# Attention scores from stacked rows of 128 built by DMA, with transposes and values moved further behind the scores

## The chip, the cores and the metric

The kernel runs on one core of one Trainium2 chip. The metric is the device time of one execution in microseconds (us), median of several runs. PE is TensorE, DVE is VectorE, ACT is ScalarE, POOL is GpSimd, SP is SyncE, which issues the DMAs.

## What is computed

A decoder trunk of two layers on a sequence of 256 tokens, width 1024, all in float32: softmax attention (16 heads of 64, partial rotary, causal inside one block of 256 tokens) and a SwiGLU feed-forward, then an mLSTM mixer (8 heads) and a second SwiGLU. Pre-norms and residual adds stand around each part. The change touches the attention alone:

```python
q = partial_rotary(qkv[0], cos, sin)
k = partial_rotary(qkv[1], cos, sin)
s_own = jnp.einsum('bhqd,bhkd->bhqk', qc, k_own, preferred_element_type=jnp.float32)
s_own = jnp.where(kpos[None, :] <= qpos[:, None], s_own, -jnp.inf)
p = jax.nn.softmax(jnp.concatenate([s_sel, s_own], axis=-1), axis=-1)
o = p @ v                                   # per head, then through w_o
```

## The kernel before

Every float32 operand is split into a high part (rounded to fp32r) and a low part (the rest), and a product is three fp32r matmuls: high by high, high by low, low by high. Weights come from HBM in units of 128x1024 (`raw`, 4 buffers), ACT casts the high part (`wh`, L150), DVE subtracts the low part (`wl`, L141).

The attention works on eight pairs of heads, hp 0 to 7. A pair goes through this chain:

- **qk**: 48 matmuls of 256 columns on PE into one PSUM bank (`pair_block`; pairs 0 and 1 come from the stage ahead). **rotary** (L473): DVE shuffles the bank into `sh` and multiplies it into `qk`, which ends the use of the bank; POOL multiplies `sh` and adds it to `qk`.
- **split_qk** (L486): ACT casts `qk` to the high half of `u`, DVE subtracts for the low half. In `u` the 64 dimensions of the pair's first head lie on partitions 0 to 63, those of the second on 64 to 127.
- **scores** (L514): 12 matmuls that contract over 64 rows, in turn for the first and the second head, into two PSUM banks.
- **softmax, exps, recip, normalize** for each head: DVE masks and takes the row maximum (`mx`, L532) and so frees the scores' bank, ACT takes the exponential (L538), DVE the reciprocal, ACT scales (`p`, L550).
- **transposes** (L555): three 128x128 transposes per head into a bank; ACT casts `ph` (L566), DVE subtracts `pl` (L569).
- **values** (L575): 12 matmuls per pair, then ACT casts `oh` (L590) and DVE subtracts `ol` (L594). The output projection `ao` reads both.

All these share four PSUM banks (`ps`); the value projection `av` and `ao` accumulate in four others (`acc`).

The order of PE, DVE and ACT in this stage is written out by the class `Stream`: it walks a list of generators (qk of pair 2, half of av, qk 3, rest of av, qk 4 to 7, then ao), each yield is one step, 92 steps in all, and a step is six matmuls of 256 columns or three of 512. Between steps it emits what is due by a position. For pair hp with s0 = `A_PAIR[hp]`, `split_qk` is due at s0 + `A_U`, the scores at s0, the transposes at s0 + `A_T`, the values at s0 + `A_V`; the pieces of the softmax follow each other by half a step to one and a half. What isn't ready in program order (`when`) is put off by half a step. The engines then run their own queues in the order of emission, so an instruction that waits holds up all behind it on its engine. The mLSTM stage has a helper, `stacks` (L434 and following), that this stage does not call: it makes `u` and copies it by six DMAs on SP into `stk`, in which a head's high and low rows lie on one set of 128 partitions, so that `dots` (L455) gets the three products out of two matmuls that contract over 128 rows.

Of the kernel before, what the change touches and what calls it, by code (L numbers as in the profile page):

```python
# [9 lines left out]
F32 = mybir.dt.float32  # L10
F32R = mybir.dt.float32r
# [5 lines left out]
P = 128  # L17
S = 256
# [8 lines left out]
LAG = 6  # L27
WARM = 16

A_PAIR = (9, 18, 27, 36, 48, 57, 65, 73)  # L30
A_U, A_T, A_V, A_W = -4, 6, 12, 1
M_START, M_STEP, M_A, M_B, M_C, M_G2, M_G3 = 32, 5, 1.5, 12, 22, 23, 28


# [33 lines left out]
def trunk_kernel(ctx: ExitStack, tc: tile.TileContext, x, w, wg, fw, tab, out):  # L68
    nc = tc.nc
# [25 lines left out]
    def ps_tile():  # L95
        return ps_pool.tile([P, 512], F32, name="ps", tag="ps")
# [79 lines left out]
    def mm(o, lhsT, rhs, start, stop):  # L176
        nc.tensor.matmul(o, lhsT=lhsT, rhs=rhs, start=start, stop=stop, skip_group_check=True)  # L177
# [96 lines left out]
    def tok_block(name, i0, n, evict, later):  # L274

        banks = [acc_tile() for _ in range(2)]
        for k in range(NF):
            if k % 2 == 0:
                u = unit(name, i0 + k // 4, k // 2 % 2)
            for t in range(2):  # L280
                wh, wl = (a[:, (k % 2) * 512:(k % 2 + 1) * 512] for a in u)
                mm3(banks[t], n.xt(k, t), (wh, wl), k == 0, k == NF - 1)
                yield
        later(evict, i0 // 2, banks)

    class Stream:
# [13 lines left out]
        def later(self, d, f, *args):  # L300
            self.at(self.pos + d, f, *args)
# [42 lines left out]
    def out_steps(acc, name, i, src):  # L344

        u, rhs = unit(name, i // 2, i % 2), src.pop(i)
        for b in range(4):
            out_tiles(acc, u, rhs, False, False, fs=(2 * b, 2 * b + 1))
            yield

    def out_start(acc, name, src):

        steps = []
        for bs in ((0, 1), (2, 3)):
            acc.extend(acc_tile() for _ in bs)
            for i in range(2):
                if bs[0] == 0:
                    steps.append((unit(name, 0, i), src.pop(i)))
                u, rhs = steps[i]
                for b in bs:  # L360
                    out_tiles(acc, u, rhs, i == 0, False, fs=(2 * b, 2 * b + 1))
                    yield
# [71 lines left out]
    def stacks(pool, mv, bufs, ubufs=2, later=None):  # L434


        u = pool.tile([P, 1024], F32R, name="u", tag="u", bufs=ubufs)
        nc.scalar.copy(u[:, 0:512], mv)
        st = pool.tile([P, 2, 768], F32R, name="stk", tag="stk", bufs=bufs)

        def rest():
            nc.vector.tensor_sub(u[:, 512:1024], mv, u[:, 0:512].bitcast(F32))
            for hh in range(2):
                r = slice(hh * 64, hh * 64 + 64)
                nc.sync.dma_start(out=st[0:64, hh].bitcast(F32), in_=u[r, 0:768].bitcast(F32))
                nc.sync.dma_start(out=st[64:128, hh, 0:512].bitcast(F32), in_=u[r, 512:1024].bitcast(F32))
                nc.sync.dma_start(out=st[64:128, hh, 512:768].bitcast(F32), in_=u[r, 0:256].bitcast(F32))

        if later is None:
            rest()  # L450
        else:
            later(rest)
        return st

    def dots(o, T, a0, na, m0, nm):  # L455
        a = T[:, 256 + a0:256 + a0 + na]
        mm(o, a, T[:, m0:m0 + nm], True, False)
        mm(o, a, T[:, 512 + m0:512 + m0 + nm], False, True)

    with ExitStack() as actx:  # L460
        ap = actx.enter_context(tc.tile_pool(name="attn", bufs=3))
# [9 lines left out]
        rq = {}  # L471
# [9 lines left out]
            nc.gpsimd.tensor_add(qk, qk, sh)  # L481
            rq[hp] = qk

        us = {}

        def split_qk(hp):  # L486

            qk = rq.pop(hp)
            u = ap.tile([P, 1024], F32R, name="u", tag="u", bufs=3)
            nc.scalar.copy(u[:, 0:512], qk)  # L490

            def low_u():
                nc.vector.tensor_sub(u[:, 512:1024], qk, u[:, 0:512].bitcast(F32))
                us[hp] = u
            main.later(1.5, low_u)

        evicted = set()

# [13 lines left out]
                evicted.add(i)  # L512

        def scores(hp):  # L514

            u = us.pop(hp)
            sc = [ps_tile() for _ in range(2)]
            for o, a0, nm in ((0, 0, P), (P, P, S)):
                for i, (al, ml) in enumerate(((0, 0), (0, 1), (1, 0))):
                    for hh in range(2):  # L520
                        r = slice(hh * 64, hh * 64 + 64)
                        mm(sc[hh][:, o:o + nm], u[r, al * 512 + S + a0:al * 512 + S + a0 + P],
                           u[r, ml * 512:ml * 512 + nm], i == 0, i == 2)
            for hh in range(2):
                main.later(0.5 + hh, softmax, 2 * hp + hh, sc[hh])

# [19 lines left out]
        pr = {}  # L546
# [5 lines left out]

        pT = {}

        def transposes(h):  # L555
            pt = pr.pop(h)
            tp = ps_tile()

            for i in range(3):
                nc.tensor.transpose(tp[:, i * P:(i + 1) * P], pt[:, i * P:(i + 1) * P], ident)  # L560
            main.later(1, halves, h, tp)

        def halves(h, tp):
            ph = ap.tile([P, 384], F32R, name="ph", tag="ph", bufs=4)
            pl = ap.tile([P, 384], F32R, name="pl", tag="pl", bufs=4)
            nc.scalar.copy(ph, tp[:, 0:384])  # L566

            def low_p():
                nc.vector.tensor_sub(pl, tp[:, 0:384], ph.bitcast(F32))  # L569
                pT[h] = (ph, pl)  # L570
            main.later(1, low_p)
# [3 lines left out]
        def values(hp):  # L575

            po = ps_tile()
            for hh in range(2):
                p = pT.pop(2 * hp + hh)
                for s, c, q in ((0, 0, 0), (1, S, P)):  # L580
                    for i, (vl, pl) in enumerate(((0, 0), (0, 1), (1, 0))):
                        mm(po[0:64, hh * S + q:hh * S + S], VT[:, s, 2 * hp + hh, vl * 64:vl * 64 + 64],
                           p[pl][:, c:c + S - q], hh == 0 and s == 0 and i == 0, s == 1 and i == 2)
            oh = ap.tile([P, S], F32R, name="oh", tag="oh", bufs=8)
            ol = ap.tile([P, S], F32R, name="ol", tag="ol", bufs=8)
            parts = [(slice(hh * 64, hh * 64 + 64), po[0:64, hh * S:hh * S + S]) for hh in range(2)]

            def high_o():
                for r, o in parts:
                    nc.scalar.copy(oh[r], o)  # L590

            def low_o():
                for r, o in parts:
                    nc.vector.tensor_sub(ol[r], o, oh[r].bitcast(F32))  # L594
                ot[hp] = (oh, ol)
            main.later(1, high_o)
            main.later(2, low_o)

        def qk(hp):
            b = ps_tile()  # L600
            yield from pair_block("aqk", hp, n, b)
            main.later(1, rotary, hp, b)
# [3 lines left out]
        main = Stream(*[(always, g) for g in (qk(2), islice(vb, 8), qk(3), vb, qk(4), qk(5), qk(6), qk(7))],  # L606
                      ((lambda: 0 in ot and 1 in ot), out_start(acc, "ao", ot)), *[((lambda hp=hp: hp in ot), out_steps(acc, "ao", hp, ot)) for hp in range(2, 7)])
        for hp in range(2):
            main.at(0, rotary, hp, banks[hp])
        main.at(0.5, v_evict, 0, banks[2:4])  # L610
        for hp, s0 in enumerate(A_PAIR):
            main.when(s0 + A_U, lambda hp=hp: hp in rq, split_qk, hp)
            main.when(s0, lambda hp=hp: hp in us, scores, hp)
            for hh in range(2):
                main.when(s0 + A_T + hh, lambda h=2 * hp + hh: h in pr, transposes, 2 * hp + hh)
            main.when(s0 + A_V, lambda hp=hp: 2 * hp in pT and 2 * hp + 1 in pT and hp // 4 in evicted, values, hp)
        with tc.manual_schedule(engines=vector_scalar):
            wlag[0], look[0] = A_W, A_LOOK
# [73 lines left out]
    with ExitStack() as mctx:  # L692
# [179 lines left out]
        def o_evict(i, banks):  # L872
# [3 lines left out]
            for t in range(2):  # L876
# [5 lines left out]
        main = Stream((always, tok_block("mv", 0, n, v_evict2, lambda *a: main.later(0, *a))), (always, tok_block("mo", 0, n, o_evict, lambda *a: main.later(0, *a))),  # L882
                      (always, tok_block("mv", 2, n, v_evict2, lambda *a: main.later(0, *a))), (always, tok_block("mo", 2, n, o_evict, lambda *a: main.later(0, *a))),
                      ((lambda: 0 in yt and 1 in yt), out_start(acc, "mout", yt)), *[((lambda h=h: h in yt), out_steps(acc, "mout", h, yt)) for h in range(2, 7)])
# [7 lines left out]
        for h in range(8):  # L892
            s0 = M_START + M_STEP * h
# [118 lines left out]
```

## Time and profile before

| | us |
|---|---|
| median of 3 runs | 610.81 (610.41 to 610.83) |
| the profiled execution, whole | 611.07 |
| its span, first to last instruction | 609.3 |
| PE busy in the span | 594.3 (98%) |
| DVE busy | 413.4 (68%) |
| ACT busy | 338.0 (55%) |
| granted PE clock, mean | 0.999 |

The page gives busy times, the chain of work that ended last (PE has 82% of it) and the costliest groups of instructions. The attention is the stretch from about 29 to 131 us. "Idle before <- X" in brackets at an instruction means that its engine stood still ahead of it until X was done. A matmul is pipelined: its own duration (0.28 us for 256 columns) is longer than the distance to the next start, which is what sets the pace.

### The profile page before, as it was taken

How to read it: one execution, taken by the hardware profiler on the slowest of the kernel's cores; microseconds unless marked ns; L12 is line 12 of the kernel's file. 1: busy time of each engine (PE TensorE's matmuls, PEld its weight loads, DVE VectorE, ACT ScalarE, POOL GpSimd, SP SyncE). 2: the span in 40 equal slices, each digit the busy share in tenths (PEclk: the TensorE clock that was granted, in tenths of full speed). 3: DMA queues.
4: the chain of work that ended last, by engine and by line, in shares of the span. 5: the costliest groups of instructions: out<-in, count | busy, mean ns of one | idle time of the engine just before them, and what ended most of it. 6: DMA issues, size and time to landing. Idle time of an engine off the chain costs nothing.

```text
span 609.3 us, 11534 instructions
## 1 busy us (share of the span) xinstructions
PE 594.3 (98%) x4588; PEld 560.4 (92%) x4588; DVE 413.4 (68%) x651; ACT 338.0 (55%) x603; POOL 71.3 (12%) x81
## 2 busy tenths in 40 slices
PE   8989899999999999999999999999999999999995
PEld 7878789999999999999999888999999999999984
DVE  5898788696966666566476678868785655656532
ACT  7657867774854444444375568846654444444412
POOL 2561023024000000000022200113200000000000
PEclk9999999999999999999999999999999999999999
DMA  8843323339665556555518868343955555555401
GB/s 311 285 156 132 138 105 134 133 124 300 212 218 197 198 187 203 186 197 198 184 41 280 258 228 232 139 139 87 308 194 177 202 175 191 188 186 195 140 1 69
DMA packets 32502, 110.10 MB, mean 181 GB/s; under 512 B 3776, under 2 KB 5568, under 8 KB 32448
## 3 DMA queue, kind: packets, MB, share of 16 engines
q1 hardware_dynamic: 32448, 109.36, 53.1%
q8 instruction: 36, 0.59, 0.4%
q14 instruction: 18, 0.15, 0.1%
HBM read 105.15 MB, written 1.05 MB: 174 GB/s over the span
## 4 chain that ended last, share of the span: by engine, by line
PE 82%; DVE 6%; ACT 6%; DMA 2%; issue 1%; POOL 1%; SPq 0%; POOLq 0%; ACTq 0%
PE ps L177 45%; PE acc L177 36%; DVE wl L141 3%; ACT wh L150 2%; DMA raw<-w 2%; ACT p L550 1%; DVE p L532 1%; ACT xh L197 1%; DVE sh L478 1%; ACT p L538 1%; POOL ssum L210 1%; PE ps L560 1%; ACT sq L209 0%; ACT oh L590 0%; DVE qk L479 0%
## 5 line engine op out<-in xcount | busy, mean ns | idle before, releaser
L141 DVE TENSOR_TENSOR wl<-raw,wh 128x1024 fp32r<-128x1024 f32 (+2 forms) x199 | 246.0, 1242 | 111.9 <-ACT wh L150 111.5
L150 ACT CAST wh<-raw 128x1024 fp32r<-128x1024 f32 (+2 forms) x199 | 205.2, 1038 | 180.9 <-PE ps L177 99.4
L177 PE MATMUL ps<-xh,wh 128*128 128x256 f32 x864 | 243.0, 281 | 2.3 <-ACT wh L150 0.9
L177 PE MATMUL ps<-xh,wl 128*128 128x256 f32 x864 | 241.4, 279 | 0.7 <-DVE wl L141 0.7
L177 PE MATMUL ps<-xl,wh 128*128 128x256 f32 x864 | 240.8, 279 | 0.0
L177 PEld LDWEIGHTS ps<-xh,wh 128*128 128x128 f32 x864 | 162.5, 188 | 4.6 <-ACT wh L150 1.1
L177 PEld LDWEIGHTS ps<-xh,wl 128*128 128x128 f32 x864 | 163.4, 189 | 1.5 <-DVE wl L141 1.4
L177 PEld LDWEIGHTS ps<-xl,wh 128*128 128x128 f32 x864 | 162.4, 188 | 0.8
L177 PE MATMUL acc<-hl,wh 128*128 128x256 f32 x176 | 48.7, 277 | 0.0
L177 PE MATMUL acc<-hh,wh 128*128 128x256 f32 x176 | 48.7, 277 | 0.0
L177 PE MATMUL acc<-hh,wl 128*128 128x256 f32 x176 | 48.7, 277 | 0.0
L210 POOL TENSOR_TENSOR ssum<-ssum,sq 128x512 f32<-128x512 f32 x12 | 20.8, 1734 | 197.9 <-issue 163.7
L634 DVE TENSOR_TENSOR tgu<-ps,R 128x512 f32<-128x512 f32 x42 | 28.6, 690 | 20.9 <-PE ps L177 20.9
L177 PE MATMUL acc<-wh,hh 128*128 128x512 f32 x88 | 34.7, 395 | 0.0
L177 PE MATMUL acc<-wl,hh 128*128 128x512 f32 x88 | 34.7, 394 | 0.0
L177 PE MATMUL acc<-wh,hl 128*128 128x512 f32 x88 | 34.4, 391 | 0.0
L177 PEld LDWEIGHTS acc<-hl,wh 128*128 128x128 f32 x176 | 33.1, 188 | 0.0
L177 PEld LDWEIGHTS acc<-hh,wl 128*128 128x128 f32 x176 | 33.0, 188 | 0.0
L177 PEld LDWEIGHTS acc<-hh,wh 128*128 128x128 f32 x176 | 33.0, 188 | 0.0
L177 PE MATMUL acc<-wh,xh 128*128 128x512 f32 x80 | 33.0, 412 | 0.0
L177 PE MATMUL acc<-wh,xl 128*128 128x512 f32 x80 | 31.6, 395 | 0.0
L177 PE MATMUL acc<-wl,xh 128*128 128x512 f32 x80 | 31.5, 394 | 0.0
(188 smaller groups left out, 855.5 us busy)
## 6 DMA issues: line engine op xcount, KB each, us to landing
raw<-w SPq DMA_DIRECT2D x195, 512.0 KB, 4.2
stk<-u SPq DMA_DIRECT2D x8, 192.0 KB, 3.3
stk<-u SPq DMA_DIRECT2D x8, 128.0 KB, 3.3
out<-yout SPq DMA_DIRECT2D x4, 256.0 KB, 2.1
XV<-x SPq DMA_DIRECT2D x7, 128.0 KB, 6.0
tab_t<-tab SPq DMA_DIRECT2D x1, 708.0 KB, 7.3
stk<-u SPq DMA_DIRECT2D x8, 64.0 KB, 2.9
fwb<-fw SPq DMA_DIRECT2D x1, 512.0 KB, 3.9
```

Source lines behind the costliest of these rows:

```text
L141: nc.vector.tensor_sub(wl[:, sl], raws[c][:, sl], wh[:, sl].bitcast(F32))
L150: nc.scalar.copy(wh[:, sl], raws[c][:, sl])
L177: nc.tensor.matmul(o, lhsT=lhsT, rhs=rhs, start=start, stop=stop, skip_group_check=True)
L197: nc.scalar.activation(self.h[:, f], X[:, f], AF.Copy, scale=wc)
L210: nc.gpsimd.tensor_add(self.ssum, self.ssum, sq)
L478: nc.vector.stream_shuffle(sh, bank, swap)
L532: nc.vector.tensor_tensor_reduce(out=pt[:, sl], in0=sc[:, sl], in1=amask[:, ms], scale=-0.125, scalar=3.0e38, op0=ALU.add, op1=ALU.min, ac ...
L538: nc.scalar.activation(pt[:, sl], pt[:, sl], AF.Exp, bias=mx[:, t:t + 1], scale=-1.0, accum_out=ss[:, t:t + 1])
L550: nc.scalar.activation(pt[:, sl], pt[:, sl], AF.Copy, scale=ss[:, t:t + 1])
L560: nc.tensor.transpose(tp[:, i * P:(i + 1) * P], pt[:, i * P:(i + 1) * P], ident)
L634: nc.vector.tensor_mul(t.rearrange("p (g t) -> p g t", g=2), bank.rearrange("p (g t) -> p g t", g=2), n.R2())
```

## The change

The attention calls `stacks` and `dots`, with six DMAs a pair on SP behind the low half of `u`. A pair's scores are then eight matmuls over 128 rows, first head, then second head. Both heads' transposes of a pair are emitted together, nine steps behind the scores (they were six and seven), values sixteen steps behind (twelve), the split eleven steps ahead of the scores (four). The scores' positions move by 3 to 7 steps. Some buffer counts shrink (`u` 3 to 2, `ph` and `pl` 4 to 3, `oh` and `ol` 8 to 7), three buffers of `stk` are added.

```diff
-A_PAIR = (9, 18, 27, 36, 48, 57, 65, 73)
-A_U, A_T, A_V, A_W = -4, 6, 12, 1
+A_PAIR = (16, 24, 32, 40, 53, 60, 68, 76)
+A_U, A_T, A_V, A_W = -11, 9, 16, 1
...
         def split_qk(hp):
-            qk = rq.pop(hp)
-            u = ap.tile([P, 1024], F32R, name="u", tag="u", bufs=3)
-            nc.scalar.copy(u[:, 0:512], qk)
-            def low_u():
-                nc.vector.tensor_sub(u[:, 512:1024], qk, u[:, 0:512].bitcast(F32))
-                us[hp] = u
-            main.later(1.5, low_u)
+            st[hp] = stacks(ap, rq.pop(hp), 3, later=lambda f: main.later(1.5, lambda: (f(), stacked.add(hp))))
...
         def scores(hp):
-            u = us.pop(hp)
+            T = st.pop(hp)
             sc = [ps_tile() for _ in range(2)]
-            for o, a0, nm in ((0, 0, P), (P, P, S)):
-                for i, (al, ml) in enumerate(((0, 0), (0, 1), (1, 0))):
-                    for hh in range(2):
-                        r = slice(hh * 64, hh * 64 + 64)
-                        mm(sc[hh][:, o:o + nm], u[r, al * 512 + S + a0:al * 512 + S + a0 + P],
-                           u[r, ml * 512:ml * 512 + nm], i == 0, i == 2)
+            for hh in range(2):
+                dots(sc[hh][:, 0:P], T[:, hh], 0, P, 0, P)
+                dots(sc[hh][:, P:384], T[:, hh], P, P, 0, S)
...
+        def turn(hp):
+            for hh in range(2):
+                transposes(2 * hp + hh)
...
             main.when(s0 + A_U, lambda hp=hp: hp in rq, split_qk, hp)
-            main.when(s0, lambda hp=hp: hp in us, scores, hp)
-            for hh in range(2):
-                main.when(s0 + A_T + hh, lambda h=2 * hp + hh: h in pr, transposes, 2 * hp + hh)
+            main.when(s0, lambda hp=hp: hp in stacked, scores, hp)
+            main.when(s0 + A_T, lambda hp=hp: 2 * hp in pr and 2 * hp + 1 in pr, turn, hp)
```

On DVE around the split of pair 6, kernel before: `p` and `mx` belong to the second head of the scores of pair 5, `wl` is a weight's low part, `ol` the outputs of pair 4, `u` the low half of pair 6's split. The rotary of pair 6 stands ahead of these rows.

```order
L532 ISA p_1241,mx_1239<-ps_1202,tab_t_109 128x128
L532 ISA mx_1239 128x1
L141 TENSOR_TENSOR wl_1192<-raw_1080,wh_1191 128x1024
L543 RECIPROCAL ss_1229<-ss_1229 128x2
L543 RECIPROCAL ss_1240<-ss_1240 128x2
L594 TENSOR_TENSOR ol_1266<-ps_1252,oh_1265 64x256 x2
L493 TENSOR_TENSOR u_1282<-qk_1216,u_1282 128x512
```

The same place in the changed kernel: `sh` and `qk` are the rotary of pair 6, `ss_1156` belongs to the softmax of pair 4, `ol` is of pair 3, and the `mx` behind the `u` is that of the first head of pair 5.

```order
L478 STREAM_SHUFFLE sh_1202<-ps_1049 128x512
L479 TENSOR_TENSOR qk_1201<-ps_1049,Cr_414 128x512
L532 RECIPROCAL ss_1156<-ss_1156 128x2
L587 TENSOR_TENSOR ol_1182<-ps_1168,oh_1181 64x256 x2
L442 TENSOR_TENSOR u_1216<-qk_1201,u_1216 128x512
L141 TENSOR_TENSOR wl_1189<-raw_1050,wh_1188 128x1024
L521 ISA p_1266,mx_1264<-ps_1242,tab_t_109 128x256
```

The low half of `u`, which needs ACT's cast of the POOL's sum, stood behind the maxima of pair 5 and now stands ahead of them.

On ACT at the same place, kernel before: exponentials of pair 5 (L538), then the cast of `u` of pair 6 (L490).

```order
L538 ACTIVATE p_1230,ss_1229<-p_1230,mx_1228 128x256
L538 ACTIVATE p_1230,ss_1229<-p_1230,mx_1228 128x128
L538 ACTIVATE p_1241,ss_1240<-p_1241,mx_1239 128x256
L538 ACTIVATE p_1241,ss_1240<-p_1241,mx_1239 128x128
L150 CAST wh_1271<-raw_1135 128x1024
L490 CAST u_1282<-qk_1216 128x512
```

And in the changed kernel: the scaling of pair 4's heads (L539) around the cast of `u` of pair 6 (L438), then the exponentials of pair 5 (L527).

```order
L539 ACTIVATE p_1146<-p_1146,ss_1145 128x128
L539 ACTIVATE p_1146<-p_1146,ss_1145 128x256
L438 CAST u_1216<-qk_1201 128x512
L539 ACTIVATE p_1157<-p_1157,ss_1156 128x128
L539 ACTIVATE p_1157<-p_1157,ss_1156 128x256
L150 CAST wh_1254<-raw_1116 128x1024
L527 ACTIVATE p_1266,ss_1265<-p_1266,mx_1264 128x256
```

The cast of `u` moved ahead of work that does not need it. In positions: pair 6's rotary is emitted at step 57 in both kernels, its split at 61 before and at 58 now.

At the end of the stage on PE, kernel before, the last rows of the values of pair 7 (`ps_1641`) are followed by ao matmuls that read the output of an earlier pair (`oh_1422`).

```order
L177 MATMUL ps_1641<-ph_1606,VT_420 64x128
L177 MATMUL ps_1641<-pl_1607,VT_420 64x128
L177 MATMUL ps_1641<-ph_1606,VT_420 64x128
L177 MATMUL acc_1324<-oh_1422,wh_1375 128x256
L177 MATMUL acc_1324<-ol_1423,wh_1375 128x256
```

In the changed kernel they are followed by those that read pair 7's own output (`oh_1726`, `ol_1727`).

```order
L177 MATMUL ps_1713<-ph_1666,VT_420 64x128
L177 MATMUL ps_1713<-pl_1667,VT_420 64x128
L177 MATMUL ps_1713<-ph_1666,VT_420 64x128
L177 MATMUL acc_1313<-oh_1726,wh_1520 128x256
L177 MATMUL acc_1313<-ol_1727,wh_1520 128x256
```

Seven steps of other matmuls, which stood between the values of pair 7 and the use of their output, now stand ahead of the values.

## Rows read from the trace of the kernel before

**Rows 1.** Stretch, us, busy (count) of PE, PEld, DVE, ACT, POOL; clock, DMA, GB/s.
```profile
29.00:131.00 102.00, 96.12 (x792) 88.00 (x791) 84.14 (x182) 72.10 (x173) 25.01 (x23) 1.00 0.40 141
```
**Rows 2.** Timeline of PE: start, duration, engine, line, operation, idle before it.
```profile
31.01 0.36 PE L177 MATMUL ps<-xh,wh 128*128 128x256 f32 x1 [0.68 <-DVE qk L479]
...
66.21 0.84 PE L560 MATMUL ps<-tab_t,p 128*128 128x128 f32 x3 [1.51 <-ACT p L550]
```
**Rows 3.** Chain that ended last, PE pieces: start, us, what.
```profile
115.80 0.33 PE ps L560 x3
...
120.58 1.05 PE ps L177 x12
121.63 7.55 PE acc L177 x66
129.19 13.60 PE ps L177 x120
...
416.17 14.13 PE ps L177 x120
```
**Rows 4.** Timeline of PE around the scores of pair 1.
```profile
47.88 0.28 PE L177 MATMUL ps<-xh,wl 128*128 128x256 f32 x1
48.09 0.96 PE L177 MATMUL ps<-u 64*128 64x128 f32 x12
...
49.20 0.28 PE L177 MATMUL ps<-xl,wh 128*128 128x256 f32 x1
```
**Rows 5.** Timeline of PE around one mLSTM head's stacked matmuls.
```profile
359.41 0.39 PE L177 MATMUL acc<-wh,xl 128*128 128x512 f32 x1
359.64 0.58 PE L177 MATMUL ps<-stk 128*128 128x256 f32 x4
...
360.34 0.40 PE L177 MATMUL acc<-wl,xh 128*128 128x512 f32 x1
```
**Rows 6.** Timelines of DVE and ACT: splits of `u`; page's row of the stack DMAs.
```profile
36.69 1.77 DVE L493 TENSOR_TENSOR u<-qk,u 128x512 fp32r<-128x512 f32 x1
...
337.57 0.69 DVE L442 TENSOR_TENSOR u<-mqk,u 128x512 fp32r<-128x512 f32 x1
...
345.17 0.62 ACT L438 CAST u<-mqk 128x512 fp32r<-128x512 f32 x1 [3.84 <-DMA stk<-u]
...
stk<-u SPq DMA_DIRECT2D x8, 192.0 KB, 3.3
```
**Rows 7.** Timelines of DVE, POOL and ACT: a rotary, and a split that waits.
```profile
82.80 0.75 DVE L478 STREAM_SHUFFLE sh<-ps 128x512 f32<-128x512 f32 x1
...
85.00 1.30 POOL L481 TENSOR_TENSOR qk<-qk,sh 128x512 f32<-128x512 f32 x1
...
35.72 0.62 ACT L490 CAST u<-qk 128x512 fp32r<-128x512 f32 x1 [2.32 <-POOL qk L481]
```
**Rows 8.** Timeline of DVE (maxima of two heads), and chain pieces.
```profile
92.08 0.42 DVE L532 CUSTOM_DVE_ANT_0 p<-ps,tab_t 128x256 f32<-128x256 f32 x1
...
93.19 2.23 DVE L141 TENSOR_TENSOR wl<-raw,wh 128x1024 fp32r<-128x1024 f32 x1
...
84.55 0.99 ACT p L538 x4
...
83.55 0.56 DVE qk L479
...
89.34 1.13 DVE wl L141
```
**Rows 9.** Timelines of ACT and DVE at the end of the attention.
```profile
121.67 0.74 ACT L590 CAST oh<-ps 64x256 fp32r<-64x256 f32 x2 [2.75 <-PE ps L177]
...
122.44 0.85 DVE L594 TENSOR_TENSOR ol<-ps,oh 64x256 fp32r<-64x256 f32 x2 [2.75 <-ACT oh L590]
...
127.18 1.37 DVE L366 TENSOR_TENSOR XV<-XV,acc 128x512 f32<-128x512 f32 x2 [0.36 <-PE acc L177]
...
128.47 0.87 DVE L198 SCALAR_TENSOR_TENSOR xl<-XV,xh 128x256 fp32r<-128x256 f32 x2
```

More of the change, by code (lines that the diff above doesn't have):

```diff
@@ L482, in rotary @@
             rq[hp] = qk
-        us = {}
+        st = {}
+        stacked = set()
         def split_qk(hp):
-            qk = rq.pop(hp)
-            u = ap.tile([P, 1024], F32R, name="u", tag="u", bufs=3)
-            nc.scalar.copy(u[:, 0:512], qk)
-            def low_u():
-                nc.vector.tensor_sub(u[:, 512:1024], qk, u[:, 0:512].bitcast(F32))
-                us[hp] = u
-            main.later(1.5, low_u)
+            st[hp] = stacks(ap, rq.pop(hp), 3, later=lambda f: main.later(1.5, lambda: (f(), stacked.add(hp))))
         evicted = set()
@@ L563, in halves @@
         def halves(h, tp):
-            ph = ap.tile([P, 384], F32R, name="ph", tag="ph", bufs=4)
-            pl = ap.tile([P, 384], F32R, name="pl", tag="pl", bufs=4)
+            ph = ap.tile([P, 384], F32R, name="ph", tag="ph", bufs=3)
+            pl = ap.tile([P, 384], F32R, name="pl", tag="pl", bufs=3)
             nc.scalar.copy(ph, tp[:, 0:384])
@@ L583, in values @@
                            p[pl][:, c:c + S - q], hh == 0 and s == 0 and i == 0, s == 1 and i == 2)
-            oh = ap.tile([P, S], F32R, name="oh", tag="oh", bufs=8)
-            ol = ap.tile([P, S], F32R, name="ol", tag="ol", bufs=8)
+            oh = ap.tile([P, S], F32R, name="oh", tag="oh", bufs=7)
+            ol = ap.tile([P, S], F32R, name="ol", tag="ol", bufs=7)
             parts = [(slice(hh * 64, hh * 64 + 64), po[0:64, hh * S:hh * S + S]) for hh in range(2)]
```

## The prediction

> **What bounds the kernel now.** I read the page first, then the busy times of the attention stretch, then the stops of PE in the timeline, then the chain. The change moves nothing outside the attention: the order of every engine is the same from the first feed of the next norm on, so the time is decided by when the first feed-forward matmul (gu0) starts. It starts at 129.19 [rows 3] and the stretch before it begins at 31.01 [rows 2], 98.2 us. PE is busy 96.12 of 102 us there, DVE 84.14, ACT 72.10 [rows 1]; a DVE that is 82% busy and runs its queue in order leaves little room, and the reader should see in rows 2 that PE's stops end with DVE or ACT (1.51 us for a scaled `p`).
>
> PE's work there without a stop: 288 qk and 192 ao matmuls at 13.60 / 120 = 0.1133 [rows 3], 54.4; 48 of 512 columns at 359.64 - 359.41 = 0.23 [rows 5], 11.0; 16 groups of transposes at 0.33, 5.3, and 8 of values at 1.05, 8.4 [rows 3]; 8 score blocks. Such a block costs, from the start of the matmul ahead to the second one behind, less two ordinary matmuls, 49.20 - 47.88 - 0.23 = 1.09 [rows 4], 8.7 in all. The sum is 87.8, so 10.4 us are stops and slower pace. The pace of a 256-column matmul has two values, 0.1133 and 14.13 / 120 = 0.1178 [rows 3]; had all 480 the slow one it would be 2.2. I take half of it, 1.0, as pace that stays, and 9.4 as stops that belong to the old order.
>
> **The scores.** Eight matmuls over 128 rows for twelve over 64. One mLSTM head of exactly this shape costs 360.34 - 359.41 - 0.46 = 0.47; of this the four matmuls take about 0.36 (two of 256, two of 128 at 0.23 for 512, rounded up), so two heads in a row 0.83 [rows 5]. Saved: 8 x (1.09 - 0.83) = 2.1 us, all on PE. Ends: 0.94 a block (two single heads, each with its edges), which saves 1.2, and 0.69 (1536 columns at 0.23 for 512, no edges), which saves 3.2; I take the value between, since the two heads follow each other.
>
> The row shows two 64-row matmuls that start almost together but a block as long as if little ran beside the other. The Trainium skill, "TensorEngine Tiling (Array Packing)", "Key Properties" and "Theoretical Speedup", says that tiles of 64 rows work in parallel, up to twice as fast, and that a change of tiling mode drains the array. By its factor alone six pairs would be 1152 columns, 0.51 us, against 1536 columns, 0.68 us, and the change would lose 8 x 0.17 = 1.4 us. The block's 1.09 us does not bear the factor out, drains and all; since both forms have rows here, it is no rival.
>
> The transposes gain nothing by standing together: six cost two times the 0.33 of three [rows 3]. Values, softmax, casts and weights are the same in number.
>
> **The stops of the new order.** I laid the new order of PE, DVE and ACT end to end by hand, with durations from the rows: 0.68 a step, two maxima 93.19 - 92.08 = 1.11, shuffle and multiply 84.11 - 82.80 = 1.3, a weight's low part 1.13, the exponentials of one head 0.99 [rows 7, 8]. Up to the low half of the first `u`, done at 36.69 + 1.77 = 38.46 [rows 6], DVE does what it did.
>
> 1. *Scores of pair 0, step 16.* They now wait for six DMAs. In the mLSTM stage DVE ended a `u` at 338.26 and the last copy of it had landed at 345.17, 6.9 us later [rows 6]; the first head's copies are issued some 1.3 to 1.9 us ahead of the last, about 5.0. So head 0 has its stack at 43.5, head 1 at 45.4. PE comes there at 31.01 + 48 x 0.1133 + 24 x 0.23 = 42.0 to 42.3. Stop 2.8. By the landing time of one DMA alone, 3.3 [rows 6], and issue, it is 0.9.
> 2. *The rotaries of pairs 4 to 7.* POOL ends 86.30 - 82.80 = 3.5 us behind the shuffle's start [rows 7]. Before, ACT's cast of `u` came four steps (2.7 us) behind the rotary and still waited (2.32 in rows 7, for pair 0). Now it comes one step behind, ahead of exponentials, `ph` casts and scalings, and the low half stands on DVE ahead of maxima. What waits on PE is the transposes, which take a PSUM bank that a maximum or a rotary on DVE must first empty. Steps 40 and 41: the next qk and the pair's four groups queue behind maximum, shuffle, multiply, maximum, 2.4 us of DVE against 1.2 of PE: 1.3. Step 49: from pair 4's shuffle 3.5 to POOL's end, 0.6 cast, 1.0 exponentials, 0.8 two casts, 0.6 `pl`, 0.7 low `u`, 2.3 two weights, 1.3 next rotary, 10.8 with hops; PE needs 9.0: 1.8. Step 53: 0.3. Step 62: the second transposes wait for pair 5's maximum behind pair 6's low `u` and a weight: 1.0. Step 69: the same with pair 7: 2.3. Together 6.7.
> 3. *Stacks again.* Scores of pairs 5 and 6 come 5 to 6 us behind their low `u`, the second head's copies 6.9: 1.5 and 0.5, 2.0.
> 4. *The end.* Values of pair 7 are emitted at step 76 + 16 = 92, behind the last step; before, seven steps (4.8 us) covered what follows. Now PE stands for the two `oh` casts, 0.74 and a hop, before the first ao matmul and for `ol`, 0.85, before the second [rows 9]: 1.0 and 0.7. DVE has two weights (2.3) queued between `ol` and the residual add; add, cast and the first `xl`, which gu0 needs, take 128.9 - 127.18 = 1.7 [rows 9], 4.0 us behind `ol` in all, while PE has 2.6 us of ao left: 1.3. Together 3.0. What hid it is gone wholly, so this is the surest term.
>
> Sum of stops 2.8 + 6.7 + 2.0 + 3.0 = 14.5, against 9.4. The other waits of the old order go: with nine steps from scores to transposes the scaled `p` is early wherever no rotary stands between. SP gets 48 issues more; the raw loads behind them come three units ahead of their cast (some 8 us) and I cost them at nothing; without that cover each group would put off a load by its issue time, 3 us.
>
> **How the numbers follow.** -2.1 + 14.5 - 9.4 = +3.0. On the profiled execution (611.07) that is 614.1; it stands 0.26 above the median 610.81, so the forecast is **613.8**, slower.
>
> **Rivals.** *Absorbed.* A stop of PE gives DVE and ACT time, so the next one is shorter. In my working most of this is in, but hops and the order of POOL against DVE are not; a weight beside POOL took 2.23 instead of 1.13 [rows 8]. If half of item 2 goes, 3.4: 610.4, no change. For it: DVE idles 18 us now; against: the waits are chains of fixed operations.
>
> *Faster.* The stacks land as single DMAs do (items 1 and 3 shrink from 4.8 to 0.9) and half of item 2 goes: 613.8 - 3.9 - 3.4 = 606.5. It decides at scores 0: if PE goes through there at 43.5 or earlier, this is the case. Against it: the 6.9 us were seen with a DMA queue no fuller than here (shares 0.40 here).
>
> *Much slower.* The SP queue: raw loads behind six copies make ACT's weight casts late, eight times 0.6: 618.6. It decides when a cast waits for a load in the middle of the stretch. For it: DVE and ACT have no slack to catch up; against: the 8 us of lead.
>
> *It does not do what it says.* `when` may put work off. In program order only the splits of pairs 5 to 7 are put off, by one step (50, 58, 66), which is in item 2; everything else falls on its number.
>
> **Chances.** Measurements of this kernel tell about 0.2% from no change, 609.6 to 612.0. Forecast (612.0 to 617) 0.62; much slower 0.06; absorbed 0.19; faster 0.13. So faster 0.13, same 0.19, slower 0.68. The range must leave out at most 0.2: from 609.5, which takes in the absorbed case, to 618.0, which takes in the upper end of the scores (3 us more than 613.8 with no gain there and a stop more).
>
> **What would show it.** Right: scores 0 stop PE near 42.3 for about 3 us on a DMA; transposes at steps 49, 62 and 69 end on DVE; ACT waits for POOL's `qk` four times, 2 to 3 us each; PE stands twice behind the last values, and the first gu0 matmul starts near 132; a score block without a wait is 0.83. Wrong: score blocks of 1.0 or more, DMA waits gone, or a stretch to gu0 that is shorter than 98.2, which would mean that the old stops were the larger sum.

## The result and the profile after

| | before | after |
|---|---|---|
| median of 13 runs each, side by side, us | 611.67 (609.94 to 615.52) | 615.99 (612.83 to 617.43) |
| ratio to before, 95% interval | | 1.0062 (1.0041 to 1.0082) |
| the profiled execution, whole | 611.07 | 616.09 |
| its span | 609.3 | 614.3 |
| PE busy in the span | 594.3 | 595.3 |
| granted PE clock, mean | 0.999 | 0.994 |

Slower by 0.62%, 3.8 us; the forecast was 613.8, 3.0 us slower than the runs it started from. The two spans differ by 5.0 us, and 4.3 of them have arisen when the first feed-forward matmul (gu0) starts. The stretch from the first matmul of the attention to that one, before and then after, columns as in [rows 1]: PE, PEld, DVE, ACT, POOL busy, clock, DMA, GB/s.

```profile
31.01:129.19 98.18, 92.98 (x770) 85.40 (x771) 80.32 (x173) 69.02 (x167) 22.40 (x16) 1.00 0.39 135
...
31.33:133.49 102.16, 92.41 (x736) 87.39 (x736) 76.30 (x172) 67.55 (x165) 24.49 (x20) 0.98 0.63 190
```

The stretch is 4.0 us longer, and PE was busy 0.6 us less in it, DVE 4.0, ACT 1.5: none of them became the bound, they wait for each other. The granted clock, 1.00 there before, is 0.98. Two of the thirteen runs had a mean clock of 0.999, like the profiled run before, and took 613.6 and 614.1 us, so this drop does not belong to every execution. Timeline of PE, the rows with idle time ahead of them, which answer to [rows 2]:

```profile
31.33 0.36 PE L177 MATMUL ps<-xh,wh 128*128 128x256 f32 x1 [0.48 <-DVE qk L479]
...
43.23 0.70 PE L177 MATMUL ps<-stk 128*128 128x128 f32 x4 [0.41 <-DMA stk<-u]
...
44.65 0.70 PE L177 MATMUL ps<-stk 128*128 128x128 f32 x4 [0.72 <-DMA stk<-u]
...
70.12 1.07 PE L553 MATMUL ps<-tab_t,p 128*128 128x128 f32 x6 [0.35 <-DVE qk L479]
...
79.45 0.52 PE L553 MATMUL ps<-tab_t,p 128*128 128x128 f32 x3 [1.34 <-ACT oh L583]
...
94.22 0.52 PE L553 MATMUL ps<-tab_t,p 128*128 128x128 f32 x3 [1.85 <-DVE mx L521]
...
104.70 0.52 PE L553 MATMUL ps<-tab_t,p 128*128 128x128 f32 x3 [2.66 <-DVE mx L521]
...
129.08 0.38 PE L177 MATMUL acc<-oh,wh 128*128 128x256 f32 x1 [0.83 <-ACT oh L583]
...
129.96 0.39 PE L177 MATMUL acc<-ol,wh 128*128 128x256 f32 x1 [0.50 <-DVE ol L587]
...
133.49 0.38 PE L177 MATMUL ps<-xh,wh 128*128 128x256 f32 x1 [0.64 <-ACT xh L197]
```

They are of three kinds: the scores of pair 0 behind the copies (43 to 45), the transposes behind DVE or ACT (70 to 105), and the end (129 to 134). The last row is the first gu0 matmul, at 133.49 where it was at 129.19. Timeline of ACT: the casts of `u` of pairs 4 to 7, all of which wait for POOL.

```profile
72.16 0.62 ACT L438 CAST u<-qk 128x512 fp32r<-128x512 f32 x1 [3.83 <-POOL qk L481]
...
81.48 0.62 ACT L438 CAST u<-qk 128x512 fp32r<-128x512 f32 x1 [2.12 <-POOL qk L481]
...
91.04 0.62 ACT L438 CAST u<-qk 128x512 fp32r<-128x512 f32 x1 [1.11 <-POOL qk L481]
...
102.65 0.62 ACT L438 CAST u<-qk 128x512 fp32r<-128x512 f32 x1 [3.37 <-POOL qk L481]
```

How the last of them reaches PE is in the chain that ended last, in order of time: start, us, what.

```profile
98.32 0.73 DVE sh L478
...
99.12 1.30 POOL sh L480
...
100.49 2.14 POOL qk L481
...
102.65 0.63 ACT u L438
...
103.30 0.05 DVE u L442
103.35 0.56 issue
103.91 0.42 DVE p L521
...
104.70 0.52 PE ps L553 x3
```

The shuffle of pair 7's rotary on DVE, its multiply and its add on POOL, ACT's cast, the low half of `u` on DVE, and only behind that the maximum of pair 6, which empties the bank that the second head's transposes want. PE needs nothing of pair 7 there.

### The profile page after: what moved, and what is told of

It reads as the page before. It is cut to its first block, busy times and chain, and to the rows that moved or that the text cites. A ratio compares the mean times of both kernels' runs of the same rounds, so it can differ in the third digit from the quotient of the medians.

```text
span 614.3 us, 11607 instructions
## 1 busy us (share of the span) xinstructions
PE 595.3 (97%) x4556; PEld 563.8 (92%) x4556; DVE 410.3 (67%) x651; ACT 337.6 (55%) x603; POOL 74.2 (12%) x81
## 4 chain that ended last, share of the span: by engine, by line
PE 84%; DVE 5%; DMA 3%; issue 3%; POOL 1%; SPq 1%; ACT 1%; POOLq 0%; DVEq 0%; ACTq 0%
PE ps L177 47%; PE acc L177 36%; DMA raw<-w 3%; DVE wl L141 2%; DMA stk<-u 1%; POOL qk L481 1%; POOL sh L480 1%; DVE sh L478 1%; PE ps L553 1%; DVE u L442 1%; DVE xl L198 1%; DVE p L521 0%; SPq L132 0%; SPq L445 0%; ACT u L438 0%
## 5 line engine op out<-in xcount | busy, mean ns | idle before, releaser
L141 DVE TENSOR_TENSOR wl<-raw,wh 128x1024 fp32r<-128x1024 f32 (+2 forms) x199 | 242.8, 1226 | 111.3 <-ACT wh L150 107.4
L150 ACT CAST wh<-raw 128x1024 fp32r<-128x1024 f32 (+2 forms) x199 | 205.2, 1038 | 185.8 <-PE ps L177 102.2
```

What stands on the lines that cost most here:

```text
L141: nc.vector.tensor_sub(wl[:, sl], raws[c][:, sl], wh[:, sl].bitcast(F32))
L150: nc.scalar.copy(wh[:, sl], raws[c][:, sl])
```

## The experiments

All were timed side by side with the kernel before. "Above after" and "below after" compare with the changed kernel: the difference of the two ratios to before, in us of 611.4, with the intervals added in squares.

**The scores from 64 rows in the new order.**

```diff
-            T = st.pop(hp)
...
+            u = us.pop(hp)
+                        mm(sc[hh][:, o:o + nm], u[r, al * 512 + S + a0:al * 512 + S + a0 + P],
```

> The changed kernel's positions, but the scores from u itself with twelve matmuls over 64 rows and no copies by DMA. Theory (the order makes the loss, the stacking is nearly free): the undisturbed score block goes from 0.93 back to 1.09 us, eight times 0.16 = +1.3, and the two DMA stops at the scores of pair 0, 0.41 + 0.72 idle (0.57 + 0.89 from start to start) = -1.5, go; together about 615.8, the same as the changed kernel within 0.2%. Rival (the copies cost: 48 issues on SP make weight loads late, and ACT and DVE with them): about 612, as the kernel before.

617.03 us, ratio 1.0092 (1.0075 to 1.0109): 1.8 us above after, plus or minus 1.7. The rival falls: without a single copy the new order is as slow or slower. The loss does not come from the stacks, their 48 issues on SP or what these delay.

**No POOL in the rotaries of pairs 4 to 7.**

```diff
-            nc.gpsimd.tensor_mul(sh3, sh3, Sr.unsqueeze(1).to_broadcast([P, 2, S]))
-            nc.gpsimd.tensor_add(qk, qk, sh)
+            if hp < 4:
+                nc.gpsimd.tensor_mul(sh3, sh3, Sr.unsqueeze(1).to_broadcast([P, 2, S]))
+                nc.gpsimd.tensor_add(qk, qk, sh)
```

> The changed kernel without POOL's two operations in the rotaries of pairs 4 to 7 (the sine half of these pairs is left out), so that the cast of u waits for DVE alone. Theory (ACT and DVE stand in their queues for POOL, and PE's transposes wait for a bank behind them): the stops of 1.50, 2.01 and 2.83 us at 79.45, 94.22 and 104.70 shrink to a few tenths, and with the last of them goes the stretch at the low clock, 1.6 us: 609 to 611. Rival (DVE's own queue, two maxima and two weights, makes these stops whatever POOL does): 614 to 616.

607.43 us, ratio 0.9938 (0.9920 to 0.9956): 7.6 us below after, plus or minus 1.7, and more than the theory asked for. ACT waits for 0.37 us at most ahead of the casts of pairs 5 to 7, the transposes' stops at steps 49, 62 and 69 (79.45, 94.22 and 104.70 in the changed kernel) are gone, and the mean clock is 0.999. With the low clock behind the last of them these stops make some 8 us, so they cover the whole gain. The stop at 70.12 is still there: it is DVE's own queue. Without POOL DVE is also quicker itself, in the weight behind the rotary of pair 7, here:

```profile
94.21 1.22 DVE L141 TENSOR_TENSOR wl<-raw,wh 128x1024 fp32r<-128x1024 f32 x1
```

and in the changed kernel, where POOL works at the same time (timelines of DVE and POOL):

```profile
99.53 1.97 DVE L141 TENSOR_TENSOR wl<-raw,wh 128x1024 fp32r<-128x1024 f32 x1
...
100.49 2.13 POOL L481 TENSOR_TENSOR qk<-qk,sh 128x512 f32<-128x512 f32 x1
```

The two together take 0.75 and 0.83 us longer than apart (1.22, and 1.30 in [rows 7]). The Trainium skill, "SBUF — State Buffer", "SBUF: two separate sides", says that DVE (with two inputs in SBUF) and GpSimd (POOL) hold a port pair by an exclusive lock, for the whole instruction. The trace agrees: DVE ends 1.1 us behind POOL's multiply (99.12 + 1.30 = 100.42), and POOL's add 1.1 us behind DVE's end, 101.50.

**The values of the last pair earlier.**

```diff
-            main.when(s0 + A_V, ...
+            main.when(s0 + (A_V if hp < 7 else 12), ...
```

> The changed kernel with the values of the last pair at step 88 in place of 92, so that four steps of ao (2.7 us) stand behind them. Theory (the tail's stops of 1.00, 0.77 and 1.2 us come from values that are emitted behind the last step): all but a few tenths of 3.0 us go, 613.0 to 613.5. Rival (the values stop at step 88 instead, because pl of the last pair is not done): 615 to 616.

612.89 us, ratio 1.0026 (1.0012 to 1.0039): 2.2 us below after, plus or minus 1.5. No stop of more than 0.35 us is left behind 105 us. The tail is a term of its own.

**The early split alone, in the kernel before.**

```diff
-A_U, A_T, A_V, A_W = -4, 6, 12, 1
+A_U, A_T, A_V, A_W = -7, 6, 12, 1
```

> The kernel before with its splits three steps earlier (2, 11, 20, 29, 41, 50, 58 and 66), so that those of pairs 4 to 7 stand none or one step behind their rotary as in the changed kernel; nothing else is changed. Theory (an early split blocks ACT and DVE behind POOL in any order): slower by 2 to 4 us, 613 to 615. Rival (it blocks only where both heads' transposes want banks that wait for a maximum, which the old order avoids): within 1 us of the kernel before, 610 to 612.

616.70 us, ratio 1.0082 (1.0066 to 1.0098): 5.0 us slower than before, by one number and with nothing else of the change. All eight splits move here. ACT's casts of pairs 5, 6 and 7:

```profile
88.58 0.62 ACT L490 CAST u<-qk 128x512 fp32r<-128x512 f32 x1 [4.22 <-POOL qk L481]
...
99.25 0.62 ACT L490 CAST u<-qk 128x512 fp32r<-128x512 f32 x1 [3.50 <-POOL qk L481]
...
109.25 0.62 ACT L490 CAST u<-qk 128x512 fp32r<-128x512 f32 x1 [2.83 <-POOL qk L481]
```

And PE behind the first of them; then the clock from 94 to 96 us (columns as in [rows 1]).

```profile
92.25 0.84 PE L560 MATMUL ps<-tab_t,p 128*128 128x128 f32 x3 [2.69 <-ACT p L550]
```
```profile
94.00:96.00 2.00, 2.00 (x11) 2.00 (x10) 2.00 (x5) 1.42 (x2) 0.00 (x0) 0.50 0.07 18
```

Here it is the scaled `p` on ACT that came late, not a bank: the same wait for POOL hits whatever stands behind it. But the loss is not that of pairs 5 to 7 alone. A stop as long stands at the first transposes, where the kernel before waited 1.00 us, and behind it, too, the clock fell (0.50 from 47 to 49 us); there the low half of pair 1's `u` stood on DVE ahead of the reciprocals of pair 0.

```profile
45.82 1.08 PE L560 MATMUL ps<-tab_t,p 128*128 128x128 f32 x3 [2.76 <-ACT p L550]
```

**The split later, in the changed kernel.**

```diff
-            main.when(s0 + A_U, lambda hp=hp: hp in rq, split_qk, hp)
+            main.when(s0 + (A_U if hp < 4 else -8), lambda hp=hp: hp in rq, split_qk, hp)
```

> The changed kernel with the splits of pairs 4 to 7 three steps later (45, 52, 60, 68), three to four steps behind their rotary; scores still from stacks. Theory (the place of the split behind POOL makes the loss): ACT comes to the cast about when POOL is done, the maxima stand ahead of the low half again, the transposes' stops at 79.45, 94.22 and 104.70 (1.50, 2.01, 2.83 and 1.6 at the low clock) mostly go and the stacks come up to 1 us late at four scores: 609 to 612. Rival (the early split was needed: the last copy lands 5.8 us behind the low half, so four scores now stop 2 to 3 us each): 616 or more.

609.59 us, ratio 0.9965 (0.9947 to 0.9983): 5.9 us below after, plus or minus 1.7, and faster than the kernel before. Timeline of DVE at the rotary of pair 7: the maximum of pair 6 now stands ahead of the low half of `u`.

```profile
94.50 0.75 DVE L478 STREAM_SHUFFLE sh<-ps 128x512 f32<-128x512 f32 x1
...
97.62 0.41 DVE L521 CUSTOM_DVE_ANT_0 p<-ps,tab_t 128x256 f32<-128x256 f32 x1
...
99.53 0.69 DVE L442 TENSOR_TENSOR u<-qk,u 128x512 fp32r<-128x512 f32 x1 [0.73 <-ACT u L438]
```

In the changed kernel it was the other way round, with DVE idle ahead:

```profile
103.30 0.69 DVE L442 TENSOR_TENSOR u<-qk,u 128x512 fp32r<-128x512 f32 x1 [1.81 <-ACT u L438]
103.91 0.42 DVE L521 CUSTOM_DVE_ANT_0 p<-ps,tab_t 128x256 f32<-128x256 f32 x1
```

The low half ends as far behind the start of the rotary's shuffle in both: 103.99 - 98.31 = 5.7 us in the changed kernel, 100.22 - 94.50 = 5.7 with the late split. For pair 4 it is 7.0 and 6.8, for pair 5 6.1 and 5.1; only pair 6 had its `u` earlier by the early split, 4.9 against 6.3. So the early split gained next to nothing, since POOL sets when `u` can be made.

**Late split and early last values together.** The two edits above in one kernel.

> The late split of the run ahead and the values of the last pair at step 88 together. Theory (tail and split are apart and add up): 2.2 us less than with the late split alone, 607 to 610. Rival (the gains overlap, since what the split gives is taken by another wait ahead of the tail): within 1 us of the late split alone.

606.38 us, ratio 0.9917 (0.9897 to 0.9937), 2.9 us below the late split alone, plus or minus 1.7. They add up, within these bounds. Two stops that were not in the changed kernel show now, 0.5 and 0.8 us, between the heads of the scores of pairs 6 and 7 (their second stack).

**Pairs 4 to 7 from 64 rows, split late.**

```diff
+            if hp < 4:
+                st[hp] = stacks(...)
+                return
...
+            main.when(s0 + (A_U if hp < 4 else -7), ...
```

> The changed kernel with pairs 4 to 7 scored from u over 64 rows, without copies, their splits seven steps ahead of the scores (46, 53, 61, 69, four to five behind the rotary), and the last values at step 88; pairs 0 to 3 as in the changed kernel. Theory: the POOL waits go (-7 to -8.5), the tail goes (-2.2), four score blocks are 0.16 longer (+0.6): 606 to 608, below the kernel before. Rival (the loss of pairs 4 to 7 comes from nine and sixteen steps of lag and from both heads' transposes together, which stay): 612 to 614.

606.15 us, ratio 0.9919 (0.9898 to 0.9940). The same as with eight stacks, late split and early last values (606.38), although the splits of pairs 4 to 7 stand one step later here: for these pairs, stacks or not makes no difference that is seen.

**No stacks at all, split late, last values early.**

> The changed positions with no stacks at all: all scores from u over 64 rows, splits of pairs 4 to 7 seven steps ahead of the scores, last values at step 88. Theory (the stacks save eight times 0.13 us of PE and cost 1.5 to 1.8 us of waiting for copies at the scores of pair 0, so nothing is left): 605 to 607.5, as the kernel with all stacks and as the one with four. Rival (the stacks save 1.8 us or more, as 617.0 against 616.0 has it): 608 or more.

607.06 us, ratio 0.9931 (0.9915 to 0.9948), 0.9 us above the kernel with eight stacks, late split and early last values, plus or minus 1.6; the splits of pairs 4 to 7 stand one step later than there. All that the stacks can be said to be worth is between -0.7 and 2.5 us.

**Only pair 0 from 64 rows.**

> The late split with the early last values, all stacked but pair 0, which is scored from u over 64 rows. Theory (the copies' latency at step 16 is on PE's path): the two stops there, 0.93 and 0.91, go and the block is 0.16 longer, 604.5 to 605. Rival (what comes behind, maxima and weights on DVE, takes their place): 606 to 606.5.

605.53 us, ratio 0.9908 (0.9888 to 0.9928): 0.6 below the kernel with eight stacks, plus or minus 1.7, which decides for neither side. The profile tells more: the two stops of that kernel (0.93 and 0.91 from start to start, less one ordinary matmul) are gone, and behind them stand these, which that kernel did not have.

```profile
49.77 0.70 PE L177 MATMUL ps<-stk 128*128 128x128 f32 x4 [0.33 <-DMA stk<-u]
...
52.51 0.52 PE L574 MATMUL ps<-tab_t,p 128*128 128x128 f32 x3 [1.01 <-DVE mx L542]
```

Counted in the same way they are 0.5 and 1.2, so 1.7 of the 1.8 us came back as other waits. By its median this is the fastest kernel; it and the other four with the new lags, a late split and early last values (606.2 to 607.2) beat both the kernel before and the changed one.

**The old lags, with stacks and late split.**

```diff
-A_U, A_T, A_V, A_W = -11, 9, 16, 1
+A_U, A_T, A_V, A_W = -11, 6, 12, 1
```

The transposes of the two heads stand apart again, too.

> The late split with the lags of the kernel before: transposes of the two heads apart, six and seven steps behind the scores, values of all pairs twelve behind (so the last pair's at step 88 too); stacks and positions of the scores as changed. To be compared with the late split with the early last values, 606.4. Theory (the longer lags buy something: with six steps PE waits for the scaled p again, as in rows 2, five such stops of 0.4 to 1.8 us in the old order): 609 to 612. Rival (the lags do nothing once the split stands right): 605.5 to 607.5.

612.22 us, ratio 1.0014 (0.9998 to 1.0030), 5.9 us above the kernel with the late split and early last values, plus or minus 1.6. The lags pay. A stop for a scaled `p` like that of [rows 2] is back, now at pair 4, and behind it the clock was at 0.50 until 99 us (timeline of PE, and a stretch with columns as in [rows 1]):

```profile
90.85 0.84 PE L553 MATMUL ps<-tab_t,p 128*128 128x128 f32 x3 [1.59 <-ACT p L539]
```
```profile
96.00:98.00 2.00, 2.00 (x11) 2.00 (x11) 2.00 (x8) 2.00 (x9) 0.00 (x0) 0.50 0.28 67
```

The chain that ended last comes to this stop from a rotary again: shuffle at 80.57, POOL to 84.90, ACT's cast of `u` at 84.92, for which ACT had waited 5.18 us, then maximum, exponentials and `p`. So what the long lags buy here is distance from that chain, and some 3 us of the profiled execution are the clock, by an estimate: half of the nearly 7 us at 0.50.

**Transposes apart, lags as changed.**

```diff
-            main.when(s0 + A_T, lambda hp=hp: 2 * hp in pr and 2 * hp + 1 in pr, turn, hp)
+            for hh in range(2):
+                main.when(s0 + A_T + hh, lambda h=2 * hp + hh: h in pr, transposes, 2 * hp + hh)
```

> The late split with the early last values, but the two heads' transposes apart as in the kernel before (nine and ten steps behind the scores); values sixteen behind as changed. Theory (it is the distance that pays, not that the transposes stand together: six cost two times the 0.33 us of three, and apart they want one bank at a time): 605 to 607.5, as with both together, 606.4. Rival (standing together is what pays, and apart brings part of the 5.8 us back that the old lags cost): 608 to 611.

607.18 us, ratio 0.9935 (0.9913 to 0.9957), 1.1 us above the kernel with the transposes of both heads together, plus or minus 1.8. It is the distance that pays; that the transposes stand together shows no gain.

**The kernel before with a later split.**

```diff
-A_U, A_T, A_V, A_W = -4, 6, 12, 1
+A_U, A_T, A_V, A_W = -3, 6, 12, 1
```

> The kernel before with its splits one step later (6, 15, 24, 33, 45, 54, 62, 70). Theory (ACT's 2.32 and 1.58 us behind POOL in the old order cost PE time too): 1 to 2 us faster, 609 to 610. Rival (those waits are covered, and the low half of u is now late for the scores three steps behind): the same or up to 2 us slower, 611 to 613.

611.79 us, ratio 1.0002 (0.9991 to 1.0013). No change, where the theory had expected 1 to 2 us. Of ACT's two waits for POOL the one of 1.58 us went and that of 2.32 stayed, the scores of two pairs wait 0.68 and 0.44 us for `u`, where those of one had waited 0.66, and those of pair 5 wait 1.23 us for a `pl` on DVE, where it had been 0.48. In the old order four steps were about right.

## Why the prediction was right, and where its terms were off

Sign, size and range held, and the main cause is the one it named. That the sum came so close is luck in part, as the table shows: terms that were too small or missing make 5.1 us, terms that were too large 4.1. The sum was made for PE's stretch from the first qk matmul of the attention to gu0: 98.2 - 2.1 + 14.5 - 9.4 = 101.2. Measured: 133.49 - 31.33 = 102.2. Term by term (a stop from start to start, less one ordinary matmul):

| term | predicted | in the trace of after |
|---|---|---|
| eight score blocks | -2.1 | -1.1 |
| item 1, copies of pair 0 | 2.8 | 1.5 |
| item 2, steps 40 and 41 | 1.3 | 1.0 |
| step 49 | 1.8 | 1.5 |
| step 53 | 0.3 | 0.2 |
| step 62 | 1.0 | 2.0 |
| step 69 | 2.3 | 2.8 |
| low clock behind step 69 | none | 1.7 |
| item 3, stacks of pairs 5 and 6 | 2.0 | 0.2 |
| item 4, up to gu0 | 3.0 | 2.7, and 0.4 at its second matmul |
| the rest: small hops and slow pace | 1.0 | 1.9 |

**Scores.** A block that nothing delays:

```profile
89.47 0.28 PE L177 MATMUL ps<-xh,wl 128*128 128x256 f32 x1
89.58 1.09 PE L177 MATMUL ps<-stk 128*128 128x128 f32 x8
90.50 0.28 PE L177 MATMUL ps<-xh,wh 128*128 128x256 f32 x1
```

From the matmul ahead to the second behind (90.62), less two ordinary ones, 0.93, and 0.98 behind values; the forecast had 0.83 and 0.94 as its end. I had put the second head at 0.36, without edges, but two heads take 90.50 - 89.58 = 0.92 from start to start, 0.46 each: the saving was mis-sized by half. By the full factor of two that "TensorEngine Tiling (Array Packing)", "Theoretical Speedup", of the Trainium skill gives as the most, the change should have lost here; the trace comes nowhere near that factor, 1.09 over 64 rows against 0.93 to 0.98.

**Item 1.** The stop is there, on a DMA, at 43.23 and 44.65, where 43.5 and 45.4 were forecast. Landing was taken from one case of the mLSTM stage. Here the low half of `u` ended at 37.03 + 1.78 = 38.81, so the two heads' copies came 4.4 and 5.8 us behind it, where 5.0 and 6.9 were forecast, and PE came later, near 42.7.

```profile
37.03 1.78 DVE L442 TENSOR_TENSOR u<-qk,u 128x512 fp32r<-128x512 f32 x1
```

What the stop is worth is less still: with it removed, most came back at the next wait.

**Item 2.** This is the cause, shown from three sides: POOL taken away in the new order, -7.6; the split later, -5.9; the early split alone in the old order, +5.0 (there in part through the first pairs). The mechanism was the forecast's, the steps too, and ACT's waits were 1.1 to 3.8 us where 2 to 3 were written. That all three transposes would end on DVE holds for steps 62 and 69; at step 49 the profile names ACT's `oh`, which ended within 0.1 us of the rotary's multiply on DVE, so which of the two held PE is open. Step 62 was put at half its size, and the clock was not in the working.

**Item 3** is the step that failed: 0.2 us where 2.0 were forecast. It was added to the other stops as if they had no effect on each other. The stops ahead (1.5 and 2.0 us) gave the copies their time; as soon as those stops were taken away, 0.5 and 0.8 us of it came up.

**Item 4** came as written, 3.0 forecast, 3.1 in the trace, 2.2 plus or minus 1.5 by its own experiment.

**The old stops.** That they would go was right: no stop for a scaled `p` is left in the changed kernel. The 9.4 that the sum gave them is a remainder, and no run measures it by itself; what is measured is that the old lags cost 5.9 us when put back into the kernel with the late split. The stretch after the attention was forecast unchanged; its order is, but gu0's matmuls fell to the slow pace, 14.28 us for 119 where 120 had taken 13.60 [rows 3], and the chain has:

```profile
134.01 14.28 PE ps L177 x119
```

That is 0.8 us for 119; why they ran so is open. With 4.0 in the stretch, 0.3 ahead of it and 0.4 at gu0's second matmul it makes 5.5, of which 0.5 came back in the mLSTM stage: the spans differ by 5.0.

**The rivals.** Faster by stacks that land early: scores 0 went through at 45.2, not at 43.5 or before, and item 2 did not halve. Absorbed: not item 2, which came to 7.5 us where 6.7 were forecast, and not item 4; item 3 was. SP's queue: one weight cast, at 41.69, had waited 2.6 us for its load, with no stop of PE that ends on it, and the order without copies is no faster.

So the change holds one part that pays (nine and sixteen steps of lag, some 6 us, the clock included), two that about break even (stacks, and transposes that stand together), and two that cost (the early split of pairs 4 to 7 some 6, the late last values 2 to 3). The smaller buffer counts for `ph`, `pl`, `oh` and `ol` stand in all the fast kernels too, so they are not the loss. With those two put right the same kernel takes 606 us, 0.8% less than before.

## What to carry to other kernels

An instruction that waits on a strictly ordered engine should stand behind all work that does not need its result: here one cast in each of four pairs, three steps too early, cost 1% of the whole kernel and made its product earlier in only one of the four. When several stops are added up, ask of each what the stops ahead of it give it in time, and test the terms of a change one at a time: a change that loses as a whole can hold a part that wins.

## What was not expected of the hardware

A stop of PE can cost more than its length. Behind the 2.66 us at 104.70 the granted clock went from 1.00 to 0.50, the lower of its two levels (1.2 for 2.4 GHz). Columns as in [rows 1]:

```profile
103.00:104.00 1.00, 0.00 (x0) 0.00 (x0) 0.70 (x2) 1.00 (x2) 0.00 (x0) 1.00 0.95 381
...
106.00:107.00 1.00, 1.00 (x7) 1.00 (x7) 0.93 (x3) 0.98 (x3) 0.00 (x0) 0.50 0.88 185
...
109.00:110.00 1.00, 1.00 (x11) 1.00 (x11) 1.00 (x3) 1.00 (x4) 0.00 (x0) 1.00 0.03 4
```

From the first to the last of the following rows of PE's timeline there are 18 starts of 256 columns, 3.70 us for what takes 18 x 0.1133 = 2.04 at the full clock:

```profile
104.97 0.37 PE L177 MATMUL acc<-oh,wh 128*128 128x256 f32 x1
...
106.11 0.41 PE L177 MATMUL acc<-oh,wh 128*128 128x256 f32 x1
106.32 0.41 PE L177 MATMUL acc<-ol,wh 128*128 128x256 f32 x1
...
108.67 0.32 PE L177 MATMUL acc<-oh,wh 128*128 128x256 f32 x1
```

The price is 1.7 us on top of 2.8. The same was seen behind the stops of 2.69 and 2.76 us of the early split in the old order; behind the 1.85 us at 94.22 the clock stayed at 1.00. The length of the stop does not decide it alone. The new order from 64 rows and the kernel with no stacks stop at nearly the same place for nearly the same time, and the clock right behind is 0.50 in the first and 1.00 in the second:

```profile
52.38 0.77 PE L562 MATMUL ps<-tab_t,p 128*128 128x128 f32 x3 [1.73 <-DVE mx L530]
...
53.00:54.00 1.00, 1.00 (x4) 0.81 (x4) 1.00 (x6) 0.88 (x4) 1.00 (x1) 0.50 0.87 348
```
```profile
52.21 0.52 PE L562 MATMUL ps<-tab_t,p 128*128 128x128 f32 x3 [1.76 <-DVE mx L530]
...
53.00:54.00 1.00, 1.00 (x6) 0.80 (x5) 1.00 (x6) 0.88 (x3) 1.00 (x1) 1.00 0.96 381
```

In the late split alone it fell behind 1.12 us, at the copies of pair 0 (0.50 from 46 to 48). What else decides is open, so 1 to 2 us of a difference between two of the kernels above can be the clock's.

The Trainium skill, "TensorE: Matmul & The Clock Gate", "Wait — 56ns, not 53.3ns?", gives a start-to-start of columns over 1.2 GHz for the lower level, by which an estimate for 256 columns is 0.213 us; the trace agrees, with 0.21 between the starts at 106.11 and 106.32. For the full clock the estimate by the same section's rule is 0.109, and the trace does not agree: 0.1133 or, in other stretches, 0.1178 [rows 3].
